# A network block of six stages on one core: activation tiles at one spacing, the first MLP's modulation sums behind its norm, four row buffers in the first attention

## The chip, the cores and the metric

One core of a Trainium2 chip runs the whole kernel. The time is in device microseconds (us), from one launch to the end of the last engine. All numbers below are of the kernel before the change, unless a row is marked as of the change.

## What is computed

256 tokens of width 1024 (float32) pass through two networks. The first: a gated branch mixer, a cross-attention to 256 memory tokens and a mixture of 16 experts. The second, two layers with modulated norms: a sparse ("NSA") attention with an MLP, then a differential attention with an MLP. Cut to what the change touches:

```python
cond = silu(c)                                   # one row of 1024
for i in range(2):
    mod = cond @ w_ada[i] + b_ada[i]             # 1024 x 6144 per layer
    sh1, sc1, g1, sh2, sc2, g2 = split(mod, 6)
    h = rms_norm(x, ln_mix_g[i]) * (1 + sc1) + sh1
    y = nsa_mixer(h, ...) if i == 0 else diff_mixer(h, ...)
    x = x + g1 * y
    h = rms_norm(x, ln_mlp_g[i]) * (1 + sc2) + sh2
    x = x + g2 * (square(relu(h @ w_mlp_in[i])) @ w_mlp_out[i])

# inside nsa_mixer: blocks of keys and values are compressed
k_cmp = rms_norm(silu(z_k @ w_ck1) @ w_ck2);  v_cmp = silu(z_v @ w_cv1) @ w_cv2
```

## The kernel before

**Products.** Activations lie transposed in SBUF, feature by token, in pairs of tiles: a high part (float32 rounded to the type `fp32r`) and a low part (the rest). `act_pair` (L183) allots a pair: for each part a tile of 8 x 256 + 32 floats per partition, tagged `aTh` or `aTl`, of which a view of 2048 floats that begins at float `at` is used. `at` is a number by hand, another one for almost every pair (2, 4, 8, 12, 16, 20, 24, 28). Weights come from HBM in 512 KB pieces (`wfetch`, L90) by SP's DMA queue, and are split by `wsplit` (L95): ACT copies the high part (`whi`, L98), DVE subtracts for the low part (`wlo`, L99). A product takes three matmuls: high by high, high by low, low by high. `mm_fm` (L137, its matmuls L140 to L142) holds 128 columns of weights in TensorE and moves 256 tokens of an activation tile past them; `mm_tm` (L144, L147 to L149) holds 128 tokens of an activation tile and moves 512 columns of weights.

**Order.** A tile framework allots the buffers, sets the waits, and reorders instructions on each engine by a scheduler that simulates a timeline. `behind(e, ins)` (L83) tells it that an instruction stands behind a fence on engine e; `norm.finish` (L297) takes the old fences off and sets new ones at the last of its high and low parts (`hilo`, L215). `wsplit` is so fenced on ACT ("A") and DVE ("V"): the splits of a block's weights stand behind the norm that the block needs. In `tick` (L198) and `skewed` (L206) pieces of generators are interleaved by hand.

**Modulation.** `mod` is summed tile by tile: 96 tiles of 128 x 1024 weights, 512 KB each, loaded by `ada_load` (L422) from the SP queue into the row buffers `ada`, taken up by `ada_mm` (L436). It has two ways. On TensorE (`ada_rows`, L431, L433): four matmuls with `cond`, a column of 128 values, as the held operand. On DVE, when it is given a pool: two instructions of 128 x 512 per tile (L451 for the first tile of a sum, L453 for the rest), which multiply by `cond` and add to `adv`. `ada_end` (L464) turns a finished row into columns `modc` (L474). `ada_step` (L479) loads a tile if none is ready and takes one up.

**The first attention** (lines 1145 to 1459, some 534 to 677 us). Its pool of row buffers `ad4` (L1153) has `B_N` = 2 tiles. `compress` (L1260) loads four weight tiles of the compression into the same buffers (`cmp_weights`, L1145), one when it needs one. After projections, 16 units `att` (L1387: 8 pairs of heads by 2 halves of the tokens) run skewed: `s` is the scores (L1395, L1398), `am` their maxima (L1402, L1403), `E` the exponentials (L1413). Between units `fill` (L1453) takes up one tile of the modulation while more than 56 are left.

**The MLPs** (`mlp`, L1464): before the norm the first block of weights and up to 8 `ada` tiles are loaded; behind the norm come 16 blocks `up` (L1476) and `down` (L1485). In the first MLP 24 more tiles of the modulation are taken up between blocks, on DVE. The second MLP has the same code and no modulation left to sum.

Of the kernel before, what the change touches and what calls it, by code (L numbers as in the profile page):

```python
# [12 lines left out]
F32R = mybir.dt.float32r  # L13
# [3 lines left out]
OP = mybir.AluOpType  # L17
AX = mybir.AxisListType

P = 128  # L20
S = 256
D = 1024
KD = 8
CH = 1024
NS2 = 8
B_N = 2
B_X, N_W, N_X = 10, 8, 8
# [5 lines left out]
EPS = 1e-6  # L33
NEG = -1e30
NOSYNC = mybir.DependencyInfo(mybir.DependencyClass.NoSync, mybir.DependencyReason.DATA)


@with_exitstack
def two_blocks_kernel(ctx, tc, A, out):
# [143 lines left out]
    def act_pair(name="aT", at=0):  # L183

        return tuple(act.tile([P, KD * S + 32], F32R, tag="aT" + c, name=name + c)[:, at:at + KD * S]
                     .rearrange("p (k q) -> p k q", k=KD) for c in "hl")
# [13 lines left out]
    def drain():  # L200
        while pending:
            tick()
# [233 lines left out]
    def ada_mm(n=1, pool=None):  # L436

        for _ in range(n):
            if not ada_ready:
                return  # L440
            i, s, kk, raw = ada_ready.pop(0)
            if kk == 0:
                ada_part.update(ps=ada_bank[:, len(ada_done) % 2, :], new=True, acc=None)
            if pool is not None:
                new = ada_part["acc"] is None
                if new:
                    ada_part["acc"] = pool.tile([P, D], F32, tag="adv", name="adv", bufs=1)
                for c in range(2):
                    acc, r = (v[:, 512 * c:512 * c + 512] for v in (ada_part["acc"], raw))
                    if new:  # L450
                        V.tensor_scalar(acc, r, cond[:, kk:kk + 1], None, op0=OP.mult)  # L451
                    else:
                        V.scalar_tensor_tensor(acc, r, cond[:, kk:kk + 1], acc, op0=OP.mult, op1=OP.add)  # L453
            else:
                ada_rows(cond[:, kk:kk + 1].to_broadcast([P, 32]), raw, ada_part["new"],
                         kk == KD - 1 and ada_part["acc"] is None)
                ada_part["new"] = False
            if kk == KD - 1:
                if ada_part["acc"] is not None:
                    ada_rows(ones[:, :32], ada_part["acc"], ada_part["new"], True)  # L460
                later(ada_end(i, s, ada_part["ps"]))
                ada_done.append((i, s))
# [35 lines left out]
    with tc.tile_pool(name="kv", bufs=1, reuse_waits="tile") as kvp:  # L498
# [18 lines left out]
        with tc.tile_pool(name="mix", bufs=1, reuse_waits="tile") as mx:  # L517
# [40 lines left out]
            g_mem, g_x, g_ffn, g_f, pscol, g_mix0, g_mix1, g_mlp0, g_mlp1 = (gc[:, 8 * j:8 * j + 8] for j in range(9))  # L558
            aM = act_pair("memT", 4)
            for t in range(2):  # L560
# [181 lines left out]

            mT = act_pair("mT", 12)
            s0s = []
# [19 lines left out]
        with tc.tile_pool(name="xa", bufs=2, reuse_waits="tile") as xp, tc.tile_pool(name="ad", bufs=B_X, reuse_waits="tile") as ad:  # L764
            log_exp()
            nx = norm(g_x, at=2)
            out_proj(mT, A["w_o"][0], nx)
# [6 lines left out]
            ada_load(N_X, ad)  # L774
            oT = act_pair("oT", 24)
            scale = 256 ** -0.5
# [103 lines left out]
    with (tc.tile_pool(name="ad3", bufs=5, reuse_waits="tile") as ad,  # L880
# [113 lines left out]
        def moe_pass(slot, okm, nx=None, pre=()):  # L994
# [8 lines left out]
            def gather(gp):  # L1003
                pr = act_pair("xg", (8, 16)[gp])
                xg.append(pr)
# [28 lines left out]
            def expert(E):  # L1034
# [19 lines left out]
                for f in range(2):  # L1054
                    T.transpose(pt[:, f * P:(f + 1) * P], sg[:, f * P:(f + 1) * P], ident)
                aT = (mp.tile([P, 2, P], F32R, tag="eah", name="eah", bufs=2),
                      mp.tile([P, 2, P], F32R, tag="eal", name="eal", bufs=2))
                split = hilo(aT[0], aT[1], pt[:, :256].rearrange("p (f q) -> p f q", f=2))
# [93 lines left out]
    with ExitStack() as st2:  # L1152
# [4 lines left out]
        if True:  # L1157
# [78 lines left out]
            if True:  # L1236
# [23 lines left out]
                def compress():  # L1260
# [7 lines left out]
                    for kv, w1 in enumerate(("nsa_w_ck1_2", "nsa_w_cv1_2")):  # L1268
                        pc = bank("cmp")
                        for half in range(2):  # L1270
                            r3 = cmp_weights(w1, half)
                            for k in range(8):
                                kt = 8 * half + k
                                behind("T", T.matmul(pc[:, :65], r3[:, k, :], Z[:, kv, 2 * kt:2 * kt + 1025:16],
                                                     start=kt == 0, stop=kt == 15))
# [49 lines left out]
                for kv, pe in enumerate(("nsa_pe_k_2", "nsa_pe_v_2")):  # L1325
# [3 lines left out]
                    T.transpose(ps[:, :16], per, ident[:16, :16])  # L1329
                    V.tensor_copy(Z[:, kv, 1024:1056:2], ps[:, :16])  # L1330
                q_block(0)
                q_block(1)
                later(compress())
# [49 lines left out]

            oT = act_pair("oT", 28)
            po = {}
# [67 lines left out]
            def fill(r):  # L1453
                tick()
                if len(ada_todo) > 56:
                    ada_step(1, ad)

            skewed([att(p_, t) for p_ in range(8) for t in range(2)], fill)
            drain()
    nx = norm(*adaln(0, 1, g_mlp0), at=16)  # L1460
# [3 lines left out]
    def mlp(i, nx, ad):  # L1464
# [7 lines left out]
        with tc.tile_pool(name="mlp", bufs=3, reuse_waits="tile") as mq:  # L1472
# [40 lines left out]
            if i == 0:  # L1513
                assert not ada_ready
                ada_load(N_D, ad)
                nx = norm(*adaln(1, 0, g_mix1), at=4)
            down((14, us[14]), (15, us[15]))
# [24 lines left out]
    with tc.tile_pool(name="ad5", bufs=4, reuse_waits="tile") as ad, tc.tile_pool(name="dif", bufs=1, reuse_waits="tile") as npl, tc.tile_pool(name="dfw", bufs=2, reuse_waits="tile") as nw:  # L1542
# [53 lines left out]
        vs = values()  # L1596
        oT = act_pair("oT", 20)
        po = {}
# [73 lines left out]
        drain()  # L1672
    nx = norm(*adaln(1, 1, g_mlp1), at=8)
    out_proj(oT, A["diff_w_out_2"][0], nx, gate(1, 0), wo, ps)
# [29 lines left out]
```

## Time and profile before

| what | value |
|---|---|
| time, median of 3 runs | 1246.94 us (1245.13 to 1247.43) |
| time of the profiled execution | 1247.1 us |
| its span | 1245.1 us |
| TensorE's clock, mean share of full speed granted | 0.98 |
| PE, busy | 1199.5 us, 96% of the span |
| DVE, ACT, busy | 889.1 us (71%), 695.5 us (56%) |
| DMA, read from HBM | 255.15 MB, 206 GB/s |

The span is what the profiler saw from the first to the last instruction; the time has 2.0 us more around it. PE is TensorE's matmuls. A matmul that is issued right behind another overlaps it, so its own duration (0.28 us for 256 columns) is longer than the distance from its start to the next start (about 0.118 us); what a matmul costs in a full stretch is that distance. The clock has two levels, and 0.50 in a stretch means that all of it ran at 1.2 GHz instead of 2.4 GHz.

### The profile page before, as it was taken

To read this page: it belongs to the slowest core of one execution; us is meant where nothing else is said; L and a number is where in the kernel's file an instruction comes from. 1 tells how busy PE (TensorE), PEld (TensorE's weight loads), DVE (VectorE), ACT (ScalarE), POOL (GpSimd) and SP (SyncE) were. 2 spreads that over 40 slices of the span, in tenths; PEclk is the share of its full clock that TensorE was granted. 3 is DMA by queue.
4 is the path that set the end of the run, shared out by engine and by line. 5 is a ranking of instruction groups with operands and counts; after the bars stand their busy time and mean duration, and the time that the engine had idled before them with its cause. 6 is when DMAs were issued, how large, how long until landed. Compare 5 with 4: busy or idle time off the path is not lost.

```text
span 1245.1 us, 22518 instructions
## 1 busy us (share of the span) xinstructions
PE 1199.5 (96%) x8762; PEld 1072.1 (86%) x8762; DVE 889.1 (71%) x1672; ACT 695.5 (56%) x1163; POOL 26.6 (2%) x34
## 2 busy tenths in 40 slices
PE   7999999999879999899999989999999999999998
PEld 6989999989667888678657889999977768999998
DVE  7999968664568999787767585487589666645443
ACT  6644447453356777566456465554566455655553
POOL 0000000000000000070000000000000000000000
PEclk9999999999879999999989989999999999999999
DMA  7665566790367999766451896687755345665651
GB/s 243 198 214 186 162 208 187 275 306 30 110 204 245 341 339 349 280 184 197 135 170 36 277 369 219 198 308 254 254 184 181 113 136 204 213 194 185 187 171 35
DMA packets 177551, 257.76 MB, mean 207 GB/s; under 512 B 14239, under 2 KB 138999, under 8 KB 177436
## 3 DMA queue, kind: packets, MB, share of 16 engines
q1 hardware_dynamic: 177436, 256.24, 62.3%
q8 instruction: 71, 1.16, 0.4%
q14 instruction: 44, 0.36, 0.1%
HBM read 255.15 MB, written 1.05 MB: 206 GB/s over the span
## 4 chain that ended last, share of the span: by engine, by line
PE 65%; DVE 3%; ACT 1%; DMA 1%; issue 1%; ACTq 0%; DVEq 0%
PE fm L141 6%; PE fm L142 6%; PE fm L140 6%; PE mo L140 5%; PE mo L141 5%; PE mo L142 5%; PE tm L147 3%; PE tm L149 3%; PE tm L148 3%; PE gu L149 2%; PE gu L147 2%; PE gu L148 2%; PE ada L433 1%; PE py L147 1%; PE py L148 1%; PE py L149 1%
## 5 line engine op out<-in xcount | busy, mean ns | idle before, releaser
L99 DVE TENSOR_TENSOR wlo<-raw,whi 128x1024 fp32r<-128x1024 f32 (+1 forms) x382 | 455.4, 1214 | 175.8 <-ACT whi L98 174.7
L98 ACT ACTIVATE whi<-raw 128x1024 fp32r<-128x1024 f32 (+1 forms) x382 | 391.8, 1048 | 273.9 <-PE fm L141 139.1
L141 PE MATMUL fm<-hTl,whi 128*128 128x256 f32 (+1 forms) x968 | 275.3, 284 | 4.5 <-DVE hTl L217 3.4
L140 PE MATMUL fm<-hTh,whi 128*128 128x256 f32 (+1 forms) x968 | 274.6, 284 | 3.2 <-ACT hTh L216 3.2
L142 PE MATMUL fm<-hTh,wlo 128*128 128x256 f32 (+1 forms) x968 | 272.8, 282 | 0.0
L141 PEld LDWEIGHTS fm<-hTl,whi 128*128 128x128 f32 (+1 forms) x968 | 183.9, 190 | 6.9 <-DVE hTl L217 5.5
L140 PEld LDWEIGHTS fm<-hTh,whi 128*128 128x128 f32 (+1 forms) x968 | 184.7, 191 | 5.6 <-ACT hTh L216 4.6
L142 PEld LDWEIGHTS fm<-hTh,wlo 128*128 128x128 f32 (+1 forms) x968 | 184.3, 191 | 0.0
L141 PE MATMUL mo<-ul,whi 128*128 128x256 f32 x512 | 143.3, 281 | 0.0
L142 PE MATMUL mo<-uh,wlo 128*128 128x256 f32 x512 | 143.1, 281 | 0.0
L140 PE MATMUL mo<-uh,whi 128*128 128x256 f32 x512 | 141.9, 281 | 0.0
L142 PEld LDWEIGHTS mo<-uh,wlo 128*128 128x128 f32 x512 | 96.6, 189 | 0.0
L141 PEld LDWEIGHTS mo<-ul,whi 128*128 128x128 f32 x512 | 96.3, 188 | 0.0
L140 PEld LDWEIGHTS mo<-uh,whi 128*128 128x128 f32 x512 | 95.7, 189 | 0.4 <-issue 0.4
L147 PE MATMUL tm<-whi,hTh 128*128 128x512 f32 x176 | 69.9, 403 | 0.7 <-ACT hTh L216 0.7
L148 PE MATMUL tm<-wlo,hTh 128*128 128x512 f32 x176 | 69.8, 398 | 0.0
L149 PE MATMUL tm<-whi,hTl 128*128 128x512 f32 x176 | 68.9, 397 | 0.0
L141 PE MATMUL fm<-oTl,whi 128*128 128x256 f32 x192 | 54.6, 286 | 0.9 <-DVE oTl L1615 0.8
L140 PE MATMUL fm<-oTh,whi 128*128 128x256 f32 x192 | 53.3, 285 | 1.4 <-ACT oTh L1614 1.3
L142 PE MATMUL fm<-oTh,wlo 128*128 128x256 f32 x192 | 53.5, 282 | 0.0
L147 PE MATMUL gu<-whi,xgh 128*128 128x512 f32 x128 | 51.4, 403 | 1.7 <-ACT xgh L1012 1.7
L628 DVE SCALAR_TENSOR_TENSOR acv<-apad,chv,acv 128x256 f32<-128x256 f32 x120 | 51.4, 478 | 0.0
(523 smaller groups left out, 2151.8 us busy)
## 6 DMA issues: line engine op xcount, KB each, us to landing
ada<-in_w_ada_dram SPq DMA_DIRECT2D x96, 512.0 KB, 5.2
raw<-in_w_mlp_in_dram SPq DMA_DIRECT2D x64, 512.0 KB, 3.6
raw<-in_w_mlp_out_dram SPq DMA_DIRECT2D x64, 512.0 KB, 4.7
raw<-in_w_in_dram SPq DMA_DIRECT2D x48, 512.0 KB, 4.0
raw<-in_w_e_down_dram SPq DMA_DIRECT2D x32, 512.0 KB, 5.4
raw<-in_w_e_gate_dram SPq DMA_DIRECT2D x61, 256.0 KB, 5.0
raw<-in_w_e_up_dram SPq DMA_DIRECT2D x61, 256.0 KB
raw<-in_diff_w_in_dram SPq DMA_DIRECT2D x24, 512.0 KB, 4.1
```

The lines of the kernel that those rows point to most:

```text
L98: behind("A", SC.activation(hi[:, :n], raw[:, :n], AF.Copy))
L99: last["lo"] = behind("V", V.tensor_tensor(lo[:, :n], raw[:, :n], hi[:, :n].bitcast(F32), op=OP.subtract))
L140: T.matmul(ps, whi[:, c:c + ncol], xh[:, xk, :], start=first, stop=False, **kw)
L141: T.matmul(ps, whi[:, c:c + ncol], xl[:, xk, :], start=False, stop=False, **kw)
L142: return T.matmul(ps, wlo[:, c:c + ncol], xh[:, xk, :], start=False, stop=last, **kw)
L147: T.matmul(ps, xh[:, xk, t0:t0 + P], w[0], start=first, stop=False)
L148: T.matmul(ps, xh[:, xk, t0:t0 + P], w[1], start=False, stop=False)
L149: return T.matmul(ps, xl[:, xk, t0:t0 + P], w[0], start=False, stop=last)
L433: behind("T", T.matmul(ada_part["ps"][32 * j:32 * j + 32, :], w, r[:, S * j:S * j + S], start=start, stop=stop, skip_group_check=True))
L628: V.scalar_tensor_tensor(acv[:, f, :], apad[:, f, j:j + S], chv[:, f, j:j + 1], acv[:, f, :], op0=OP.mult, op1=OP.add)
```

## The change

Four things, by the lines of the kernel before:

1. **Spacing and shifts.** The tiles of `act_pair` grow from 2080 to 2304 floats per partition. The pairs `memT`, `xg` and the norm ahead of the differential attention now start at float 0, as the norm ahead of the first attention did; every other pair starts at 8 or 16. The expert's pair `ea` (L1056) becomes a tile of 288 floats with a shift of 8. With tiles of 2304 floats the high and the low part of a pair lie 18,432 bytes apart in both buffers of the tag; before, it was 16,896 and 16,768, since another tile that shares the tag `aTh` sets the size of that slot.
2. **Modulation sums behind the norm.** L451 and L453 get `behind("V", ...)`.
3. **First attention.** `B_N` is 4. The four tiles of the compression are loaded between the blocks of queries, ahead of `compress`. Four `ada` tiles are loaded before the units begin; `fill` takes up one tile if one is there, and tops the buffers up; what is left is taken up at the end.
4. `dynamic_dma_scratch_size=1024` is given to the program.

```diff
-B_N = 2
+B_N = 4
+EA = 8
...
     def act_pair(name="aT", at=0):
-        return tuple(act.tile([P, KD * S + 32], F32R, tag="aT" + c, name=name + c)[:, at:at + KD * S]
+        return tuple(act.tile([P, KD * S + 256], F32R, tag="aT" + c, name=name + c)[:, at:at + KD * S]
...
                     if new:
-                        V.tensor_scalar(acc, r, cond[:, kk:kk + 1], None, op0=OP.mult)
+                        behind("V", V.tensor_scalar(acc, r, cond[:, kk:kk + 1], None, op0=OP.mult))
                     else:
-                        V.scalar_tensor_tensor(acc, r, cond[:, kk:kk + 1], acc, op0=OP.mult, op1=OP.add)
+                        behind("V", V.scalar_tensor_tensor(acc, r, cond[:, kk:kk + 1], acc, op0=OP.mult, op1=OP.add))
...
-            aM = act_pair("memT", 4)
+            aM = act_pair("memT")
-            mT = act_pair("mT", 12)
+            mT = act_pair("mT", 8)
-            nx = norm(g_x, at=2)
+            nx = norm(g_x, at=8)
-            oT = act_pair("oT", 24)
+            oT = act_pair("oT", 16)
-                pr = act_pair("xg", (8, 16)[gp])
+                pr = act_pair("xg")
...
-                aT = (mp.tile([P, 2, P], F32R, tag="eah", name="eah", bufs=2),
-                      mp.tile([P, 2, P], F32R, tag="eal", name="eal", bufs=2))
+                aT = tuple(mp.tile([P, 2 * P + 32], F32R, tag="ea" + c, name="ea" + c, bufs=2)[:, EA:EA + 2 * P]
+                           .rearrange("p (f q) -> p f q", f=2) for c in "hl")
...
-                            r3 = cmp_weights(w1, half)
+                            r3 = cw.pop(0)
...
+                cw = [cmp_weights("nsa_w_ck1_2", half) for half in range(2)]
                 q_block(0)
+                cw += [cmp_weights("nsa_w_cv1_2", half) for half in range(2)]
                 q_block(1)
...
-            oT = act_pair("oT", 28)
+            oT = act_pair("oT", 16)
...
             def fill(r):
                 tick()
-                if len(ada_todo) > 56:
-                    ada_step(1, ad)
-
+                if ada_ready:
+                    ada_mm(1)
+                ada_load(min(B_N - len(ada_ready), len(ada_todo) - 56), ad)
+
+            ada_load(B_N, ad)
             skewed([att(p_, t) for p_ in range(8) for t in range(2)], fill)
+            ada_mm(len(ada_ready))
...
-                nx = norm(*adaln(1, 0, g_mix1), at=4)
+                nx = norm(*adaln(1, 0, g_mix1))
-        oT = act_pair("oT", 20)
+        oT = act_pair("oT", 16)
-    nx = norm(*adaln(1, 1, g_mlp1), at=8)
+    nx = norm(*adaln(1, 1, g_mlp1), at=16)
...
-    nc = _bacc.Bacc("TRN2", target_bir_lowering=False, num_devices=1)
+    nc = _bacc.Bacc("TRN2", target_bir_lowering=False, num_devices=1, dynamic_dma_scratch_size=1024)
```

The order of instructions differs in two places only: the first attention and the start of the first MLP. Everywhere else each engine has the same order, with other addresses.

DVE at the start of the first MLP, before: from the norm's products `h` (x by its scale; `nr`) on, with the low parts `hTl` and the sums `adv` between them; the last `hTl` and the first split `wlo` come behind the rows shown.

```order
L451 TENSOR_SCALAR adv<-ada,cond 128x512 x2
L309 TENSOR_SCALAR h<-h,gA,modc 128x256
L217 TENSOR_TENSOR hTl<-h,hTh 128x256 x2
L453 SCALAR_TENSOR_TENSOR adv<-ada,cond,adv 128x512 x2
L305 TENSOR_TENSOR h<-xT,nr 128x512 x2
L217 TENSOR_TENSOR hTl<-h,hTh 128x512
L453 SCALAR_TENSOR_TENSOR adv<-ada,cond,adv 128x512 x2
L309 TENSOR_SCALAR h<-h,gA,modc 128x256
L453 SCALAR_TENSOR_TENSOR adv<-ada,cond,adv 128x512
L217 TENSOR_TENSOR hTl<-h,hTh 128x512
L453 SCALAR_TENSOR_TENSOR adv<-ada,cond,adv 128x512 x2
L217 TENSOR_TENSOR hTl<-h,hTh 128x512
```

The same place with the change (its lines are one higher).

```order
L310 TENSOR_SCALAR h<-h,gA,modc 128x256
L218 TENSOR_TENSOR hTl<-h,hTh 128x256
L306 TENSOR_TENSOR h<-xT,nr 128x512
L218 TENSOR_TENSOR hTl<-h,hTh 128x256
L218 TENSOR_TENSOR hTl<-h,hTh 128x512
L306 TENSOR_TENSOR h<-xT,nr 128x512
L310 TENSOR_SCALAR h<-h,gA,modc 128x256
L218 TENSOR_TENSOR hTl<-h,hTh 128x512 x2
L452 TENSOR_SCALAR adv<-ada,cond 128x512 x2
L100 TENSOR_TENSOR wlo<-raw,whi 128x1024
L454 SCALAR_TENSOR_TENSOR adv<-ada,cond,adv 128x512 x2
L100 TENSOR_TENSOR wlo<-raw,whi 128x1024
```

The sums now stand behind the last `hTl`; one tile's two instructions stand ahead of the first `wlo`, a second tile's two ahead of the second.

PE where the units of the first attention begin, before: `ada` are tiles of the modulation (four matmuls each), `ax` small products and transposes of the projection's end, and behind them come the first scores.

```order
L433 MATMUL ada<-ada,cond 32x256 x4
L1349 MATMUL ax<-Bk,qT 128x32 x16
L433 MATMUL ada<-ada,cond 32x256 x4
L1317 MATMUL ax<-w_8097,hv 128x64 x4
L433 MATMUL ada<-ada,cond 32x256 x4
L1189 MATMUL ax<-ident,kd_8317 128x128 x4
L433 MATMUL ada<-ada,cond 32x256 x4
L1189 MATMUL ax<-ident,kd_8378 128x128 x4
L1370 MATMUL ax<-ident,Sc 128x128 x4
L433 MATMUL ada<-ada,cond 32x256 x4
L1370 MATMUL ax<-ident,Sc 128x128 x4
L433 MATMUL ada<-ada,cond 32x256 x4
```

The same place with the change.

```order
L434 MATMUL ada<-ada,cond 32x256 x4
L1352 MATMUL ax<-Bk,qT 128x32 x16
L434 MATMUL ada<-ada,cond 32x256 x6
L1318 MATMUL ax<-w_8105,hv 128x64 x4
L434 MATMUL ada<-ada,cond 32x256 x3
L1190 MATMUL ax<-ident,kd_8317 128x128 x4
L434 MATMUL ada<-ada,cond 32x256 x11
L1190 MATMUL ax<-ident,kd_8378 128x128 x4
L434 MATMUL ada<-ada,cond 32x256 x4
L1373 MATMUL ax<-ident,Sc 128x128 x4
L434 MATMUL ada<-ada,cond 32x256 x4
L1373 MATMUL ax<-ident,Sc 128x128 x4
```

By the third unit's first score, 12 tiles of the modulation (counted from the first row shown) stand ahead instead of 9, and one tile stands directly ahead of it instead of two. Of the 17 tiles counted from there 5 are left behind that point instead of 8.

## Rows read from the trace of the kernel before

**Rows 1.** The page: PE and the other engines over the span; the DMA queue.

```profile
PE 1199.5 (96%) x8762; PEld 1072.1 (86%) x8762; DVE 889.1 (71%) x1672; ACT 695.5 (56%) x1163; POOL 26.6 (2%) x34
...
q1 hardware_dynamic: 177436, 256.24, 62.3%
```

**Rows 2.** Stretches, PE: 24 us of each MLP; us, PE busy (instructions), clock, DMA share, GB/s.

```profile
716.80:740.80 24.00, 20.86 (x142) 0.79 1.00 365
1055.60:1079.60 24.00, 23.73 (x194) 1.00 0.52 176
```

**Rows 3.** Timeline, DVE, first MLP: start us, us, instruction xcount, [idle before <-releaser].

```profile
716.23 0.87 DVE L451 TENSOR_SCALAR adv<-ada,cond 128x512 f32<-128x512 f32 x2
...
719.69 1.41 DVE L453 SCALAR_TENSOR_TENSOR adv<-ada,cond,adv 128x512 f32<-128x512 f32 x2 [1.59 <-DMA ada<-in_w_ada_dram]
...
727.06 0.68 DVE L217 TENSOR_TENSOR hTl<-h,hTh 128x512 fp32r<-128x512 f32 x1
727.66 1.22 DVE L99 TENSOR_TENSOR wlo<-raw,whi 128x1024 fp32r<-128x1024 f32 x1
```

**Rows 4.** Timeline, DVE, second MLP: the first two wlo splits behind the same norm.

```profile
1060.90 2.36 DVE L99 TENSOR_TENSOR wlo<-raw,whi 128x1024 fp32r<-128x1024 f32 x2 [0.26 <-ACT whi L98]
```

**Rows 5.** Timeline, PE, second MLP: the first matmul behind the norm.

```profile
1055.70 0.38 PE L140 MATMUL fm<-hTh,whi 128*128 128x256 f32 x1 [1.12 <-ACT hTh L216]
```

**Rows 6.** Stretches, PE, first attention.

```profile
618.00:626.00 8.00, 6.78 (x41) 0.58 0.61 192
...
632.40:636.40 4.00, 3.96 (x21) 0.57 0.65 213
636.40:650.00 13.60, 13.60 (x125) 1.00 0.48 143
```

**Rows 7.** Chain of waits, first attention: start us, us, what.

```profile
610.04 0.57 PE ada L433 x8
...
622.08 1.01 PE ada L433 x8
```

**Rows 8.** Timeline, PE, first attention: the third unit starts.

```profile
632.44 0.72 PE L433 MATMUL ada<-ada,cond 128*32 128x256 f32 x8 [2.06 <-DMA ada<-in_w_ada_dram]
633.09 0.58 PE L1395 MATMUL s<-kTd,qrT 128*128 128x256 f32 x1
```

**Rows 9.** Timeline, DVE, then ACT: reductions and exponentials of the first units.

```profile
629.00 1.99 DVE L1402 TENSOR_REDUCE am<-s 128x2 f32<-128x256 f32 x4 [0.87 <-PE s L1398]
...
632.20 0.37 ACT L1413 ACTIVATE E<-s,am 128x128 f32<-128x128 f32 x1
```

**Rows 10.** Stretches and tiles, `ada`: PE (records, clock, DMA share, GB/s); SP issues.

```profile
609.90:626.80 16.90, 4.81 (x48) 0.80 0.54 161
626.80:633.00 6.20, 1.84 (x24) 0.99 0.70 212
...
L428 SPq DMA_DIRECT2D ada<-in_w_ada_dram x16: 327/328/372, 610.7 to 662.2; - x16
```

**Rows 11.** Stretches, PE: only matmuls of 256 columns (bar two transposes).

```profile
263.90:271.00 7.10, 7.10 (x61) 1.00 0.64 214
740.00:800.00 60.00, 60.00 (x512) 1.00 0.69 229
1031.00:1047.00 16.00, 16.00 (x136) 1.00 0.93 328
1100.00:1160.00 60.00, 60.00 (x509) 1.00 0.61 192
```

**Rows 12.** Timeline, PE: matmuls of 512 columns, first and last of 14, twice.

```profile
603.46 0.39 PE L148 MATMUL tm<-wlo,hTh 128*128 128x512 f32 x1
...
606.70 0.39 PE L147 MATMUL tm<-whi,hTh 128*128 128x512 f32 x1
...
930.10 0.40 PE L147 MATMUL tm<-whi,hTh 128*128 128x512 f32 x1
...
933.16 0.40 PE L148 MATMUL tm<-wlo,hTh 128*128 128x512 f32 x1
```

## Prediction

> **What bounds the kernel now.** I read the page first. PE is busy for 1199.5 us of 1245.1, and DVE, ACT and the DMA queue for far less [rows 1]: only what shortens PE's stream or its gaps can move the time. The chain of waits says where PE isn't the end of the chain; two places lie where the change edits. One is the start of the first MLP. The stretch view over the first 24 us behind its norm, beside the same 24 us of the second MLP, is the best witness of this case: same code, same shapes, and 142 matmuls against 194, at a mean clock of 0.79 against 1.00 [rows 2]. The reader is to see why in DVE's timeline: an `adv` product stands between the norm's own instructions, and the next waits 1.59 us for a DMA while `h` and `hTl` queue behind it; the norm's last `hTl` starts at 727.06 [rows 3]. The second MLP has no sums, and its splits begin 5.2 us behind its first matmul [rows 4, 5]. The other place is the first attention: half clock in two stretches [rows 6], and a third unit that starts behind a 2.06 us wait for a row buffer [rows 8]. Elsewhere PE is full, and what counts is the distance of one matmul from the next [rows 11, 12].
>
> The sum is made against the profiled execution's 1247.1 us, which lies 0.2 above the median (1246.94).
>
> **(a) The sums behind the norm: -4.5.** The change's order takes all `adv` products out of the norm and puts two ahead of each of the first two splits. Without them the first MLP would be its twin: 52 matmuls more in 24 us, by 0.118 (60.00/507; a window also counts the one or two at its edges, [rows 11]) 6.1 us. Given back: the sums moved. In the twin the second split ends at 1060.90 + 2.36 = 1063.26, 7.56 us behind the first matmul (1055.70) [rows 4, 5]. With 0.87 for the first tile's halves and 1.41 for the next tile's [rows 3] it ends 9.84 us behind it. Queued behind these products are only splits (and their readers on PE); `up(1)` needs the second split 60 matmuls behind the norm: 60 x 0.118 = 7.1, and the 1.1 us of small gaps that the twin has too (24.00 - 194 x 0.118, [rows 2]), is 8.2. PE waits 9.84 - 8.2 = 1.6 us, so -6.1 + 1.6 = -4.5. Bounds: -6.1, if the splits are early enough after all; -3.4, if the second split is needed at 7.1 us (9.84 - 7.1 = 2.7). The sums' total on DVE is unchanged. The `ada` tiles are taken up later, their buffers come free later, and SP's queue can hold MLP weights behind a load that waits for one. That costs nothing while the weights run ahead: the MLP needs one 512 KB piece per 24 matmuls (2.8 us), and one takes 1.44 us at 365 GB/s [rows 2]; without that cover each piece that is late costs up to 1.44 us.
>
> **(b) The first attention: -5.8.** Three steps.
> - The third unit's start. Its `s` begins at 633.09 behind the DMA wait [rows 8]. With four buffers the tile ahead of it should lie there. What is late next is the exponentials of unit 0, which free its banks: the last ends at 632.20 + 0.37 = 632.57, so 0.5 us by itself. These start earlier too: four reductions (1.99 us) stood ahead of the first unit's `am` product, now two [rows 9]: -1.0. Ahead of it PE ran at 0.58 of the clock from 618 to 626 [rows 6]; an `ada` tile took 1.01 us there and 0.57 at full clock [rows 7]. PE carries the chain in about 5.2 of these 8 us, so full clock would give up to 5.2 x 0.44 = 2.3. More tiles sit in PE's gaps now, but its gap ahead, which waits for DVE's `kTl` work, stays: I take 0.9. Sum -2.4, between -0.5 and -3.8.
> - The half clock from 632.4 to 636.4 follows this wait. Without it 4.0 x 0.43 = -1.7 [rows 6]; with another wait there, 0.
> - 12 tiles instead of 9 are summed ahead of the third unit, in gaps: PE has 4.81 us of `ada` in 16.9 [rows 10] and idle time there. Behind, PE is full (13.60 of 13.60, [rows 6]), so three tiles less give 3 x 0.57 = -1.7 [rows 7].
>
> Sum -5.8, between -2.2 and -7.2. It stands if 12 tiles can be there: 4 are loaded ahead, 8 more from 610.7 on (the first of 16 issues, [rows 10]). At 1.44 us each that is 11.5 us, by 622.
>
> Cost nothing: the four compression tiles are loaded two blocks early, past three loads of projection weights on SP's queue. PE's stream there is like that of the cross-attention, full at a DMA share of 0.64 [rows 11], so the queue has room; if the weights weren't fetched far enough ahead, 1 MB before either block is 2.9 us at 365 GB/s. The scratch size: all movement goes by the hardware queue [rows 1]. The shift of `ea` and the larger tiles are places, not work.
>
> **(c) The addresses: -2.5.** What an address costs no row tells by itself; the distance between starts differs by place. 256 columns: less two at the edges, 60.00/510 = 117.6 ns in the first MLP, 60.00/507 = 118.3 in the second; 16.00/134 = 119.4 in the differential output, 7.10/59 = 120.3 in the cross-attention [rows 11]. If one spacing brings each place to the pace of the best: second MLP 0.6% of 175 us is -1.0; differential output 192 x 1.8 ns = -0.35; cross-attention 192 x 2.7 = -0.5. Where the activation is held and 512 columns move, the first attention (no shift) has 3.24/14 = 231.4 ns, the differential attention (shifted) 3.06/13 = 235.4 [rows 12]; 384 like those shifted by 4 ns is -1.5. Sum -3.4. All other tiles move too, the MLPs' `u` among them, 1536 matmuls which would lose 2.5 us at about the differential output's pace (119.6 for 118.0). Bounds: -4.5, if the 1 us for tiles not listed here (`mem`, mixer) comes on top, and +2.5, if only the MLPs' loss comes; I take -2.5.
>
> The rule against this is in the Trainium skill, "TensorE: Matmul & The Clock Gate", Part 2, "Step-by-step: what each phase is for": TensorE reads SBUF through two independent ports, so loading the next weights takes nothing from the running matmul. By that rule (c) is 0; the differing paces of [rows 11] speak against it, though without saying that the address is their cause.
>
> **Sum: -4.5 - 5.8 - 2.5 = -12.8, so 1234.3 us.**
>
> **Rivals.**
> - *Addresses do nothing* (0.18): the places differ by their DMA load instead (shares 0.61 to 0.93 in [rows 11]; the slow 1031 us stretch has the highest, but the cross-attention at 0.64 is slowest). 1247.1 - 10.3 = 1236.8. The rule of the page above would make it so.
> - *The attention gains nothing* (0.11): in the 6.2 us before the third unit the queue moved 212 GB/s [rows 10], 2.5 us a tile; 8 tiles are then 20 us, from 610.7 to 630.7, where they are now. Against: with two buffers the queue idled between. 1247.1 - 7.0 = 1240.1.
> - *The clock falls again in the first MLP* (0.07): the lost 0.21 of 24 us, up to 5.0 us [rows 2], stays lost although DVE is quicker. Against: the twin has the same 1.12 us wait [rows 5] and holds 1.00. 1234.3 + 5.0 = 1239.3.
> - *Slower* (0.14): the spacing of 18,432 bytes, now the same in both buffers, lands badly for the 256-column matmuls, some 5,600 of which move an activation tile (counted from the loops). (a) and (b) give 10.3 us, and 10.3/5600 = 1.8 ns more for each eats them: 119.8 instead of 118.0, a pace which the cross-attention already exceeds [rows 11]. At 121 ns: 5600 x 3.0 = +16.8, in all +6.5, 1253.6. For it speaks only that such paces occur; against it, that most places are at 117.6 to 118.3 now with two different spacings.
> - *The stalls only move* (0.05): the attention waits for its fifth tile, the first MLP for its second split, and 11 us of the 12.8 come back: 1245.3, within the bound of no change.
>
> **How the numbers follow.** My forecast has 0.45, the rivals 0.18, 0.11, 0.07, 0.14, 0.05. A measurement can tell 0.2% (2.5 us) from no change. Faster are the forecast and the first three rivals: 0.81. The slower rival decides from 1.8 ns on; around that point it is no change (0.04), above it slower (0.10). With the stalls that only move: same 0.09, slower 0.10. Range: best bounds -6.1 - 7.2 - 4.5 = -17.8, 1229.3, and 1 us lower for the scatter of the runs (1245.13 to 1247.43); worst of the forecast -3.4 - 2.2 + 2.5 = -3.1, 1244.0. So 1228 to 1244, which holds the first three rivals too.
>
> **What would show it.** (a) Some 180 or more matmuls in the 24 us behind the first MLP's norm, clock 1.00, no `adv` before the last `hTl`, and a wait of about 1.6 us for the second `wlo`. (b) No DMA wait at the third unit, no half clock around it, and fewer `ada` records behind it. (c) 118 ns or less in all four stretches of rows 11, and 231 to 232 in the differential attention. I am wrong if (c) shows 119 or more in the MLPs, if `ada` loads land every 2.5 us in the attention, or if the `wlo` splits of the first MLP trail PE for longer than two blocks.

## The result, and the profile after

The changed kernel takes **1232.91 us** (median of 4 runs, 1230.13 to 1233.73) where the kernel before takes 1247.18 in the same comparison (1245.13 to 1248.14): a ratio of 0.9872, 95% interval 0.9853 to 0.9892, or 14.3 us. A second comparison, made with the experiments, has 0.9868 (0.9847 to 0.9889). The forecast was 1234.3 in a range from 1228 to 1244. Its profiled execution took 1230.13, the lowest of its runs, with a span of 1228.1, so the profile shows more gain (17.0) than the medians.

The page, in the places of [rows 1]:

```profile
PE 1183.5 (96%) x8762; PEld 1061.1 (86%) x8762; DVE 888.9 (72%) x1672; ACT 696.2 (57%) x1163; POOL 26.6 (2%) x34
...
q1 hardware_dynamic: 177436, 256.24, 63.1%
```

PE is busy for 16.0 us less; the other engines have the work they had. As each of the two kernels was profiled a second time, the stages can be set beside each other with their scatter. The table is worked out from the start times of PE's instructions (us; first profile, second profile):

| stage, by PE's starts | before | changed |
|---|---|---|
| start to the experts' router | 325.15, 325.24 | 324.18, 324.17 |
| experts | 192.58, 191.98 | 187.75, 189.21 |
| first attention's projection | 87.33, 87.36 | 86.56, 86.56 |
| first attention: its last projection matmul to the output projection | 68.62, 67.82 | 65.58, 68.02 |
| output projection and norm | 38.60, 38.60 | 38.58, 37.84 |
| first MLP, to its first `mo` matmul | 19.08, 17.43 | 13.73, 14.09 |
| from there to the end | 505.05, 506.16 | 503.00, 502.68 |

The means differ by 14.5 us in all: 4.3 at the start of the first MLP, 1.4 in the attention, and 8.8 in the other stages, where little but addresses changed (in the projection also when the compression's tiles are loaded).

**The first MLP.** PE's stretches, as in [rows 2]: 24 us from the first matmul behind the norm.

```profile
707.17:731.17 24.00, 22.99 (x186) 1.00 1.02 378
1039.20:1063.20 24.00, 23.28 (x191) 1.00 0.52 176
```

186 matmuls instead of 142, at full clock in this execution. DVE's timeline, as in [rows 3], and two rows of PE's:

```profile
711.48 0.69 DVE L218 TENSOR_TENSOR hTl<-h,hTh 128x512 fp32r<-128x512 f32 x1 [0.46 <-ACT hTh L217]
712.09 0.88 DVE L452 TENSOR_SCALAR adv<-ada,cond 128x512 f32<-128x512 f32 x2
712.88 1.22 DVE L100 TENSOR_TENSOR wlo<-raw,whi 128x1024 fp32r<-128x1024 f32 x1
714.02 1.41 DVE L454 SCALAR_TENSOR_TENSOR adv<-ada,cond,adv 128x512 f32<-128x512 f32 x2
715.35 1.22 DVE L100 TENSOR_TENSOR wlo<-raw,whi 128x1024 fp32r<-128x1024 f32 x1
```

```profile
707.23 0.39 PE L141 MATMUL fm<-hTh,whi 128*128 128x256 f32 x1 [1.12 <-ACT hTh L217]
...
716.62 0.39 PE L143 MATMUL fm<-hTh,wlo 128*128 128x256 f32 x1 [0.78 <-DVE wlo L100]
```

The norm's last `hTl` starts 4.25 us behind PE's first matmul; before, it was 10.2 us (716.86 to 727.06). Two instructions of the sums stand ahead of each of the first two splits, and PE waits 0.78 us for the second.

**The first attention.** PE's stretches for [rows 6], here 611 to 640:

```profile
611.00:619.00 8.00, 5.15 (x58) 1.00 0.88 297
622.40:626.40 4.00, 3.72 (x35) 1.00 0.95 308
626.40:640.00 13.60, 13.60 (x108) 1.00 0.35 120
```

Full clock in all three. The third unit, as in [rows 8], with no wait ahead of it, and what PE waited for ahead of the units (us in total, times, longest). The last of the rows is the first matmul of the output projection:

```profile
623.37 0.64 PE L434 MATMUL ada<-ada,cond 128*32 128x256 f32 x8
623.93 0.39 PE L1398 MATMUL s<-kTd,qrT 128*128 128x256 f32 x1
...
668.66 0.39 PE L141 MATMUL fm<-oTh,whi 128*128 128x256 f32 x1
```

```profile
PE ada L434 <- DMA ada<-in_w_ada_dram: 2.2, 3, 1.2
PE ax L1190 <- DVE Vc L1322: 0.7, 1, 0.7
```

The DMA wait of [rows 8] is not gone; it stands ahead of the first scores now, 2.2 us in three pieces where it was 3.8 in two. The sums of the modulation behind the third unit are fewer: 40 records where there were 64, at 8 records a tile.

**The paces.** A pace is the mean distance from the start of a matmul to the start of the next, in ns; where the text says "by PE's start times", it is taken over a whole stretch of one kind of matmul, without the waits in it. Stretches for [rows 11] and timeline rows for [rows 12] (14 intervals, 13 intervals):

```profile
263.15:270.25 7.10, 7.10 (x62) 1.00 0.81 292
728.00:788.00 60.00, 60.00 (x513) 1.00 0.73 248
1015.00:1031.00 16.00, 16.00 (x138) 1.00 0.94 328
1083.50:1143.50 60.00, 60.00 (x513) 1.00 0.60 191
```

```profile
596.05 0.40 PE L148 MATMUL tm<-whi,hTh 128*128 128x512 f32 x1
...
599.24 0.39 PE L150 MATMUL tm<-whi,hTl 128*128 128x512 f32 x1
...
913.48 0.39 PE L148 MATMUL tm<-whi,hTh 128*128 128x512 f32 x1
...
916.43 0.39 PE L149 MATMUL tm<-wlo,hTh 128*128 128x512 f32 x1
```

Less two at the edges, 256 columns now take 118.3, 117.4, 117.6 and 117.4 ns, and 512 columns 3.19/14 = 227.9 and 2.95/13 = 226.9 ns, both below the 231.4 that I had taken for the floor.

### The profile page after: what moved, and what is told of

The parts are those of the page before. It is cut to its first block, busy times and chain, and to the rows that moved or that the text cites. A ratio compares the mean times of both kernels' runs of the same rounds, so it can differ in the third digit from the quotient of the medians.

```text
span 1228.1 us, 22512 instructions
## 1 busy us (share of the span) xinstructions
PE 1183.5 (96%) x8762; PEld 1061.1 (86%) x8762; DVE 888.9 (72%) x1672; ACT 696.2 (57%) x1163; POOL 26.6 (2%) x34
## 4 chain that ended last, share of the span: by engine, by line
PE 64%; DVE 3%; ACT 2%; issue 1%; DMA 1%; ACTq 0%; DVEq 0%
PE fm L142 6%; PE fm L143 6%; PE fm L141 6%; PE mo L141 5%; PE mo L142 5%; PE mo L143 5%; PE tm L148 3%; PE tm L150 3%; PE tm L149 3%; PE gu L150 2%; PE gu L148 2%; PE gu L149 2%; PE ada L434 1%; PE o L1449 1%; PE py L148 1%
## 5 line engine op out<-in xcount | busy, mean ns | idle before, releaser
L141 PEld LDWEIGHTS fm<-hTh,whi 128*128 128x128 f32 (+1 forms) x968 | 182.2, 188 | 5.6 <-ACT hTh L217 4.6
```

Source lines behind the costliest of these rows:

```text
L141: T.matmul(ps, whi[:, c:c + ncol], xh[:, xk, :], start=first, stop=False, **kw)
```

## The experiments

All times are against the kernel before in the same comparison; us by the ratio of 1247. In the edits, lines are cut to the part that changes, and of like lines one or two are shown.

| kernel | ratio (95% interval) | us |
|---|---|---|
| e1_sums: the sums alone | 0.9971 (0.9956 to 0.9986) | -3.6 |
| e2_att: the attention alone | 0.9986 (0.9970 to 1.0002) | -1.7 |
| e3_addr: the addresses alone | 0.9948 (0.9929 to 0.9968) | -6.5 |
| e4_noshift: changed, all shifts 0 | 0.9965 (0.9949 to 0.9981) | -4.4 |
| e5_shift8: changed, 8 for 16 | 0.9920 (0.9899 to 0.9940) | -10.0 |
| e6_shift: before, new shifts | 0.9968 (0.9952 to 0.9984) | -4.0 |
| e7_late: changed, sums later | 0.9881 (0.9856 to 0.9906) | -14.8 |
| e8_bn5: changed, five buffers | 0.9879 (0.9854 to 0.9904) | -15.1 |
| e9_light: changed, light sums | 0.9868 (0.9838 to 0.9898) | -16.5 |
| e10_both: e7 with 8 in three places | 0.9898 (0.9874 to 0.9922) | -12.7 |
| the changed kernel again | 0.9868 (0.9847 to 0.9889) | -16.5 |

**1. The sums alone** (before, with this):

```diff
-V.tensor_scalar(acc, r, cond[:, kk:kk + 1], None, op0=OP.mult)
+behind("V", V.tensor_scalar(acc, r, cond[:, kk:kk + 1], None, op0=OP.mult))
-V.scalar_tensor_tensor(acc, r, cond[:, kk:kk + 1], acc, op0=OP.mult, op1=OP.add)
+behind("V", V.scalar_tensor_tensor(acc, r, cond[:, kk:kk + 1], acc, op0=OP.mult, op1=OP.add))
```

> Only the modulation sums go behind the norm. If the parts act by themselves and add (my theory), the first MLP's start is as in the changed kernel: some 186 matmuls in the 24 us behind the norm, clock 1.00, and 4.5 to 5.5 us less (about 1242). If the first MLP gains only because the attention ahead of it hands over its buffers and its clock in another state (rival), the clock falls again there and the gain is under 2.5 us.

Measured: 1242.8 us, 3.6 less by the ratio; the MLP's start takes 13.73 us, as in the changed kernel, with no fall of the clock there and the same wait for the second split:

```profile
PE fm L140 <- ACT hTh L216: 1.1, 1, 1.1
PE fm L142 <- DVE wlo L99: 0.7, 1, 0.7
```

That is less than the 4.5 to 5.5 expected, which the interval (1.8 to 5.5) still reaches. The part stands by itself; the rival falls. Over all profiles the clock fell at this place in all five with the sums inside the norm, for 3.4 to 10.2 us, and in one of the nine with the sums behind it (second profile of the changed kernel, 3.4 us).

**2. The attention alone** (before, with the attention's edits and the small scratch, without which two more buffers have no room):

```diff
-B_N = 2
+B_N = 4
-r3 = cmp_weights(w1, half)
+r3 = cw.pop(0)
+ada_load(B_N, ad)
...
+dynamic_dma_scratch_size=1024
```

> Only the first attention's part, with the smaller scratch that makes room for the two buffers. My prediction was 5.8 us less (about 1241). The trace of the changed kernel shows some 3 to 3.5 us between the first modulation tile of that stage and the output projection; if that is the part's own worth (theory: waits for DVE take the place of the three tiles removed), about 1244; if the rest of the predicted gain was eaten by the addresses or by the run (rival), 1241.

Measured: 1245.26, 1.7 less, with an interval that just reaches no change: less than either number. Its trace shows one reason. The clock fell in the stretch ahead of the units, which it did not in the first profile of the changed kernel:

```profile
611.40:618.20 6.80, 6.80 (x41) 0.50 0.36 98
```

It fell in the second profile of the changed kernel too, though later in the stage. PE's stretches, of the first profile and then of the second, the same program, which stood 1.5 us later at this place; the rows on either side begin at the same point of the program:

```profile
607.20:615.20 8.00, 6.34 (x69) 1.00 0.66 194
615.20:622.00 6.80, 5.62 (x60) 1.00 0.91 336
```

```profile
608.70:616.70 8.00, 6.06 (x65) 1.00 0.68 196
616.70:623.50 6.80, 6.19 (x38) 0.50 0.85 309
```

PE was busy for 6.34 of the 8 us in one and for 6.06 in the other, and once the clock falls (616.7, for 6.8 us), once it doesn't. Over all profiles (but e8, with five buffers, and e9, which leaves work out): with the order of before the stage took 68.6, 67.8, 68.4, 68.6 and 68.1 us, and its clock fell there in all five; with four buffers it took 65.6, 65.8, 64.9 and 65.6 where the clock held, 66.5 where it fell for 3.4 us, and 68.0 and 67.8 where it fell for 6.8. So the stage is nearly 3 us shorter where the clock holds, and half a microsecond where it falls for as long as before. What is lost again lies ahead of the scores: 9 tiles stand there instead of 6, and from the last projection matmul to the first score it took 18.7 and 19.2 us with four buffers where the clock fell for 6.8 us, against 16.2 to 17.2 with the order of before.

**3. The addresses alone** (before, with the tiles of 2304 floats, the new shifts, the expert's pair and the small scratch).

```diff
-KD * S + 32
+KD * S + 256
-act_pair("mT", 12)
+act_pair("mT", 8)
-act_pair("oT", 24)
+act_pair("oT", 16)
...
+dynamic_dma_scratch_size=1024
```

> Only addresses: spacing, shifts, the expert's pair and the smaller scratch. Predicted 2.5 us less (1244.5). The two traces differ by some 6 us ahead of the attention and 2 behind the first MLP, which would be 8 us less (1239). If the truth lies in the medians of the whole change (14.3 less, of which 5.3 and 3.2 go to the other parts), 5 to 6 us less, 1241.5. If addresses do nothing (rival), 1247 within 2.5 us, and the paces of 256 and 512 columns are as before.

Measured: 1240.21, 6.5 less. The paces are those of the changed kernel, place by place (by PE's start times 227.0 to 228.5 ns where the activation is held, from 231.5 to 234.6; 116.7 in the two projections of the cross-attention's side that got a shift of 8, from 117.8 and 119.5). Of the 6 us that the first two traces differ ahead of the attention, some were one execution's waits among the experts: the first profile of before has 192.6 us there, those of e1 and e2, which have the old shifts and spacing, 190.0 and 189.8. The small scratch isn't what sets the paces: e2 has it with the old tiles, and its paces are those of before (234.6 ns in the memory projection, 233.5 in the differential attention).

**4. The changed kernel without shifts.**

```diff
-[:, at:at + KD * S]
+[:, 0:KD * S]
-EA = 8
+EA = 0
```

> The changed kernel with all shifts at 0 and the new tile sizes. If the distance between the moving tile and the weights' tile counts (theory), the 256-column matmuls slow by 1 to 2 ns where they had a shift of 8 or 16: 3 to 10 us more than the changed kernel (1236 to 1243). If only the spacing of high and low part counts (rival), the same as the changed kernel within 2 us.

Measured: 1243.71, a ratio 0.009 to 0.010 above that of the changed kernel, 11 to 12 us: more than I had expected. PE's stretches in the mixer (256 columns throughout) of the changed kernel, and of the one without shifts there and in the first MLP:

```profile
130.00:170.00 40.00, 40.00 (x344) 1.00 0.53 165
```

```profile
130.00:170.00 40.00, 40.00 (x337) 1.00 0.52 164
728.00:788.00 60.00, 60.00 (x508) 1.00 0.81 281
```

344 against 337 matmuls in 40 us. At a shift of 0 all ten stretches that move a tile of `act_pair` run at 119.8 to 120.1 ns by PE's start times, which is the pace of my slower rival; in the first profile of the changed kernel those at 8 and 16 run at 116.7 to 117.8. The shift, not the distance between high and low part, makes this difference.

**5. The changed kernel again, and a shift of 8 for 16.** The second profile is used above.

> The changed kernel once more, for a second profile and more times. If the stage differences between the two first profiles belong to the change (theory for the first MLP and the paces), they come back: first MLP some 5.3 us shorter, moving tiles at shift 8 at 116.7 ns, at shift 16 at 117.3 to 117.8. What does not come back (rival: scatter of one execution) I expect in the experts' stage, where kernels without any change of addresses were already 1.5 us shorter than the first profile, in the half clock of the attention, and in the output projection behind it.

> The kernel before once more, one look: the same paces by place as in its first profile to 0.2 ns if the addresses set them (theory); the experts' stage 1.5 to 3 us shorter than in the first profile if that was one execution's waits.

Measured: 1232.48 for the changed kernel, one run of 1245.05 for the one before; the paces of the changed kernel by place came back within 0.5 ns, with one exception below. Those of before did not all come back to the 0.2 ns expected: the projection of the cross-attention had 119.5 and then 118.5 ns, the differential attention 233.5 and 234.1. The experts took 192.0 us in the second profile of before, so the scatter there is between kernels and executions, 189.8 to 192.6.

```diff
-norm(*adaln(0, 1, g_mlp0), at=16)
+norm(*adaln(0, 1, g_mlp0), at=8)
-norm(*adaln(1, 1, g_mlp1), at=16)
+norm(*adaln(1, 1, g_mlp1), at=8)
-act_pair("oT", 16)
+act_pair("oT", 8)
```

> The changed kernel with a shift of 8 floats where it had 16 (two MLPs, three attention outputs). If the distance to the weights sets the pace (theory), these 2,070 matmuls go from 117.7 to 116.7 ns: 2 us less than the changed kernel. If any shift that isn't 0 gives the same (rival), no difference.

Measured: 1238.0, some 6 us more than the changed kernel. The matmuls that got the shift did as expected (116.7 to 116.9 ns), but for the cross-attention's output (117.6, where it had 117.4). But the MLPs' second products, whose own addresses are the same in both kernels, slowed. PE's timeline, first matmul of a `down` and first of the next `up`, 48 apart, of the changed kernel and of this one:

```profile
1097.52 0.28 PE L141 MATMUL mo<-uh,whi 128*128 128x256 f32 x1
...
1103.16 0.28 PE L141 MATMUL fm<-hTh,whi 128*128 128x256 f32 x1
```

```profile
1101.32 0.28 PE L141 MATMUL mo<-uh,whi 128*128 128x256 f32 x1
...
1107.08 0.28 PE L141 MATMUL fm<-hTh,whi 128*128 128x256 f32 x1
```

5.64/48 = 117.5 ns against 5.76/48 = 120.0. Over 1536 matmuls this is some 3.5 us (the first MLP's went to 119.6), where the shift gave some 2. The profile, one of its faster executions, shows no more than this net loss of some 1.5 behind the norm of the first MLP (518.4 us to the end against 516.7); where the rest of the 6 us is spent was not settled.

**6. The shifts alone**, on the kernel before with its old spacing.

```diff
-act_pair("memT", 4)
+act_pair("memT")
-act_pair("mT", 12)
+act_pair("mT", 8)
-act_pair("xg", (8, 16)[gp])
+act_pair("xg")
...
```

> The kernel before with the new shifts alone: old spacing of 16,896 and 16,768 bytes, old expert pair. If the shift alone does it (theory, by the kernel without shifts, which lost it all), nearly all of the 6.5 us that the addresses gave: 4.5 to 6.5 less than before, with the paces of the changed kernel. If the common spacing is needed too (rival), less than 2.5 us.

Measured: 1244.02, 4.0 less (2.0 to 6.0), between my two numbers. The times alone do not tell it from e3 (6.5, 4.0 to 8.8); the paces do: the spacing makes a difference where the activation is held. PE's timeline in the differential attention, 13 intervals:

```profile
922.95 0.40 PE L148 MATMUL tm<-wlo,hTh 128*128 128x512 f32 x1
...
925.95 0.40 PE L149 MATMUL tm<-whi,hTl 128*128 128x512 f32 x1
```

230.8 ns: the shift of 0 takes 235.4 [rows 12] to 231, the spacing takes it to 226.9. One execution speaks against the spacing as the only way there: e1 has the addresses of before, and the first 120 of the 288 matmuls of this place ran at 226.7 ns in it, where before and e2 have 233 to 236 (13 intervals):

```profile
920.07 0.39 PE L149 MATMUL tm<-whi,hTl 128*128 128x512 f32 x1
...
923.02 0.39 PE L148 MATMUL tm<-wlo,hTh 128*128 128x512 f32 x1
```

The kernel of e6 has the attention's order of before, and in its profile the clock did not fall a second time at the third unit (the last row is the first matmul of the output projection, and behind it the same row of the kernel before):

```profile
630.60 0.39 PE L1395 MATMUL s<-kTd,qrT 128*128 128x256 f32 x1
...
632.55 0.33 PE L1430 MATMUL pz<-ident,E 128*128 128x128 f32 x1 [0.37 <-DVE E L1419]
...
634.94 0.64 PE L433 MATMUL ada<-ada,cond 128*32 128x256 f32 x8 [0.36 <-DMA ada<-in_w_ada_dram]
...
675.36 0.39 PE L140 MATMUL fm<-oTh,whi 128*128 128x256 f32 x1
```

```profile
678.26 0.38 PE L140 MATMUL fm<-oTh,whi 128*128 128x256 f32 x1
```

From the third unit to the output projection it took 44.76 us, and 45.11 in e1, whose clock didn't fall there either. The changed kernel took 44.73 (623.93 to 668.66), the one before 45.17 (633.09 [rows 8] to 678.26). The other profiles agree: 45.2 in the two more in which the clock fell there (second profile of before, e3), and 44.7 in all with four buffers and whole sums. At full clock PE waits behind the third unit, first for DVE's `E` and then for the next modulation tile; at half clock neither wait is there.

**7. Later sums, five buffers, light sums**, all three on the changed kernel.

```diff
+                        if j == 1:
+                            fence["V"] = last["lo"]
                         if len(ada_ready) > (ADA_A if left else 0):
```

> The changed kernel with the modulation sums of the first MLP also behind the splits of its second block. PE waits some 0.9 us for that block's second split there. If the sums ahead of it are the cause (theory), the wait goes and the first MLP's start is 0.8 to 1 us shorter (1231.5 by time). If the sums then hold buffers and with them the weights' loads (rival), the wait comes back later in the same MLP and the time is the same or up to 2 us more.

```diff
-B_N = 4
+B_N = 5
-tag="per", name="per", bufs=2
+tag="per", name="per", bufs=1
```

> The changed kernel with five row buffers in the first attention (the room comes from a second buffer of a small tile). In four profiles PE waited 2.0 to 2.2 us for modulation tiles ahead of the first scores. If too few tiles lie ready there (theory), one more takes 1 us of these waits and the stretch from the end of the projection to the first scores falls to 15.5 us or less; 1 to 2 us in all. If the clock's fall in that stretch decides (rival: it fell in some profiles of kernels with four buffers and not in others, 19.2 and 18.7 us against 16.1 to 16.9), the median moves only if the fall becomes rarer, and the profile shows one of the two values.

```diff
-ada_part["ps"][32 * j:32 * j + 32, :], w, r[:, S * j:S * j + S]
+ada_part["ps"][32 * j:32 * j + 32, :ada_part.get("n", S)], w, r[:, S * j:S * j + ada_part.get("n", S)]
+ada_part["n"] = 64
```

> The changed kernel with a quarter of the columns in each modulation matmul of the first attention, which leaves out three quarters of those sums. My prediction took the tiles behind the third unit as PE time at full price: 5 tiles of 0.57 us, of which three quarters go, 2.1 us less from the third unit to the output projection (44.7 to 42.6). If PE waits there for DVE and ACT anyway, and the tiles lie in these waits (theory), under 0.7 us less there (44.0 or more), and little ahead of it, since the waits are for DVE's work and for DMA.

What PE waited for at the MLP's start in e7, and ahead of the attention's units in e8:

```profile
PE fm L141 <- ACT hTh L217: 1.1, 1, 1.1
```

```profile
PE ada L434 <- DMA ada<-in_w_ada_dram: 3.4, 4, 1.3
```

In e7 the wait for the second split is gone: PE's 100th matmul behind the norm starts 12.8 us after the first, against 13.7 in the changed kernel, as expected. From PE's first matmul of the MLP to the end its profile has 515.4 us against 516.7 and 516.8; the time (1233.26) doesn't tell this from the changed kernel. In e8 the wait for tiles is longer, 3.4 us in four pieces, as 11 tiles instead of 9 are taken up ahead of the first scores; the stretch to the first scores took 18.7 us at full clock, and the time (1233.54) is no better: the theory of too few tiles falls, and so does the rival. In e9 the third unit's first score and the output projection begin at

```profile
622.98 0.39 PE L1398 MATMUL s<-kTd,qrT 128*128 128x256 f32 x1 [0.45 <-ACT E L1416]
...
666.73 0.39 PE L141 MATMUL fm<-oTh,whi 128*128 128x256 f32 x1
```

43.75 us apart, 0.95 less than 44.7, and I had set 0.7 as the limit of my theory. Six light tiles stand behind the third unit there instead of five whole ones, 0.9 us of PE's work instead of 2.9 (at 0.57 a whole tile, a quarter of it for a light one): a little under half of the tiles' price is paid behind the third unit.

**8. Both small gains.**

```diff
+                        if j == 1:
+                            fence["V"] = last["lo"]
...
-act_pair("oT", 16)
+act_pair("oT", 8)
```

> The kernel with the late sums of the first MLP, and a shift of 8 in place of 16 in the three attention outputs only (the MLPs keep 16, since their second products slowed when it was 8). If the pace of an output's stretch hangs on its own shift (theory), 576 matmuls go from 117.5 to 116.8 ns, 0.4 us, with the late sums' 1.2 us some 1.5 less than the changed kernel (1231). If a stretch behind them takes another pace, as the MLPs' second products did (rival), up to 2 us more than the changed kernel.

Measured: 0.9898 (0.9874 to 0.9922); the three outputs run at 116.8 to 117.6 ns and no stretch behind them changed, but the time is the changed kernel's within the intervals. No run here is shown to beat the changed kernel.

## Why the prediction was right

The total was right, 12.8 us forecast and 14.3 measured, but of its three terms one held and two were off in opposite directions, each by 4 us: that the sum came out so near is luck in part. The parts alone add up to 11.8 us, which their intervals don't tell from 14.3; whether they help each other was not settled.

- **(a), -4.5: held.** Alone it gave 3.6 us (1.8 to 5.5). The twin told the size: 44 of the 52 matmuls came back. The second split ends 715.35 + 1.22 - 707.23 = 9.34 us behind the first matmul, where I had worked out 9.84, and the wait was 0.78 instead of 1.6. The rival of the falling clock came up in one execution (second profile, 3.4 us at 712) without undoing the gain.
- **(b), -5.8: too large.** Alone it gave 1.7 (from 3.7 less to 0.2 more). The third unit came 2.1 us sooner behind the first (6.22 to 4.15 us), near the 2.4 of the first step. What failed is the second and third step: "The half clock from 632.4 to 636.4 follows this wait. Without it 4.0 x 0.43 = -1.7" and "three tiles less give 3 x 0.57 = -1.7". The stretch behind the third unit became 0.45 us shorter, not 3.4. In e1 and e6, with the order of before and no second fall, it took 45.1 and 44.8: the half clock cost 0.1 to 0.4, since at full clock waits for `E` and for the next tile take its place, and the three tiles brought no more than 0.4. The third step also put the three tiles at nothing ahead of the units, "in gaps"; with the clock fallen alike, PE needed some 2 us more up to the first score. PE being full behind the unit was no proof that it was the limit: it was slow enough to cover those waits. The changed kernel has such waits too (0.3 us for `E`, 0.5 for `oTl`). The rival that the attention gains nothing is not excluded by e2's time. Its reason was wrong: with four buffers the queue moved 336 GB/s from 615.2 to 622.0, 1.6 us for a 512 KB tile and not 2.5, and 12 tiles were summed ahead of the third unit. But waits for tiles moved ahead of the first scores, 2.2 us, and the clock still fell there in four of nine profiles with the new order.
- **(c), -2.5: too small.** Alone it gave 6.5 (4.0 to 8.8). The step that was mis-sized is "384 like those shifted by 4 ns is -1.5". I took the 231.4 ns of the unshifted attention for the floor; the common spacing took all four places that hold activations to 227 to 228 ns, that attention's own projection too. By PE's start times: memory projection 22.52 to 21.79 us, experts 92.26 to 90.94, first attention 57.53 to 56.71, differential attention 68.54 to 67.04, together 4.4. Of this, the differential attention's 1.5 is the least sure, as e1 was 1 us shorter there with the old addresses. The 256-column places did about as I had summed them (second MLP 0.9 for 1.0, differential output 0.35, cross-attention 0.4 for 0.5); the one that lost is `memT`, now at shift 0, from 118.1 to 120.0 ns.

The rule of two independent read ports, from the Trainium skill's "TensorE: Matmul & The Clock Gate", Part 2, "Step-by-step: what each phase is for", gave 0 for (c); the addresses alone gave 6.5 us, and the shifts taken away cost 11. So (c) is not 0; whether the weight loads have a part in it, of which the rule speaks, or what else in TensorE or SBUF makes the difference, no run here shows.

The slower rival was real as a mechanism: at the new spacing without shifts every stretch that moves a tile of `act_pair` runs at the 119.8 ns that I had named as the point from which it decides. Its price was too high: the MLPs' second products kept 117.5 ns, the held activations gained, and that kernel (e4) is still 4.4 us faster than the one before. The shifts of 8 and 16 avert it.

## What to carry to other kernels

Where the same code runs twice in a kernel under two conditions, its twin is a good price for a change: here it gave 4.5 us, and the part alone 3.6 by the times and some 4.3 by the stage. A full engine is not always the limit: before work is priced as time off a full stretch, look at what it would wait for without that work. Where operand tiles start and how far apart they lie was worth 0.5% of this kernel's time (e3), and the shifts taken away cost 0.9% (e4); set them by trials on whole stages, as one stage's setting can change the next one's pace.

## What the runs showed of the hardware

- **The pace of a stretch is not set by its own addresses alone.** In e5 the second products of the MLPs went from 117.5 to 120.0 ns with operand addresses that the edit leaves as they were, when the products ahead of them went from 117.8 to 116.7. And one program has two paces in two executions: the first attention's output projection, in 10 us of the changed kernel's first profile and of its second:

```profile
684.00:694.00 10.00, 10.00 (x87) 1.00 0.86 297
```

```profile
685.00:695.00 10.00, 10.00 (x91) 1.00 0.78 252
```

87 against 91 matmuls, at full clock; over the whole projection 117.7 against 113.6 ns by their start times. Many stretches keep to one value for a hundred matmuls and more: 116.7, 117.8 and 120.0 ns are seen in many places, 113.3 (also in e3) for longer only in this projection; in e2 it changed between 122.2 and 117.8 twice. What chooses between them stays open.
- **The clock's fall in the attention is a matter of the execution**: with the same program, PE busy for 6.06 of the 8 us ahead of the fall and for 6.34 of 8 at the same place of the other profile, it fell to 1.2 GHz for 6.8 us in one and not in the other. That stage took 68.0 us against 65.6.
